# Keys and queries of three attention stages: loads moved from GpSimd's queue, with a cast, to SyncE's queue as plain float32, rows outermost

## The chip, the cores and the metric

One Trainium2 chip, one of its cores. The time is the device time of one execution in microseconds (us). Before the change the median of three runs is 3687.04 us (3684.84 to 3689.37).

## What is computed

Two transformer blocks on a sequence of 1024 rows of width 1024, all in float32. The first has latent attention (8 heads), dilated attention (8 heads) and a mixture of 16 experts; the second has two layers, each with differential attention (4 heads), grouped-query attention (6 heads over 2 key heads) and neighbourhood attention (6 heads), over 1024 grid rows and 256 context rows. Cut to what the change touches, which is the operands of the score products:

```python
def mla_attention(q, k, v):            # first block; k and q have 64 + 32 columns
    s = einsum('bqhd,bkhd->bhqk', q_blk, k) * scale
    return einsum('bhqk,bkhd->bqhd', softmax(s), v)
...
def dilated_branch(q, k, v, dilation, half):   # first block, three dilations
    s = einsum('brnqhd,brnkhd->brnhqk', qb, kb) * (Dh ** -0.5)
...
def second_block(...):                 # for each of 2 layers
    oa = diff_attend(qa, ka_all, va_all, lam)              # kind A
    yb = gqa_attend(qb, kb_all, vb_all) * silu(gb)         # kind B
    yn = neighbourhood_attend(qn, kn, vn, kn_c, vn_c, nat_rpb[l], rows) * silu(gn)   # kind C
    x = x + gt * (concatenate([ya, yb, yn]) @ w_out[l])
```

## The kernel before

TensorE multiplies float32 as sums of products of rounded parts: each operand is split into a high part and a rest, both of a type called float32r, which has the bits of a float32. The projections before an attention stage write their split, transposed queries and keys into HBM tensors `self.st[key]` ("stacks": Mk, Mq, Mr, Dk, Dq for the first block, Ak, Aq, Bk, Bq, Ck, Cq for a layer of the second). A stack is laid out as [part a (high, rest), block of heads, row, column], so a row of keys is 1024 or 1280 floats long (4 or 5 KB) and the two parts of a row lie far apart.

There are three attention stages: `attn1` (about 330 to 820 us of the profiled span), and `attn2` for layer 0 (about 2010 to 2570 us) and for layer 1 (about 3080 to 3570 us). In each a plan (`Plan`) simulates the engines ahead of time, with a cost for each operation written in the code, and issues operations in the order of the simulated time. An operation has a priority, a dictionary of the engines that may do it with its cost on each, the operations that it depends on and the buffers that it needs; it takes the first engine of the dictionary that is free. A load is such an operation: it takes the time given on the queue that issues it, and its data arrive after a modelled transfer. All instructions of an engine are chained in the order of the plan, those of SyncE (SP) alone are not (`Plan.issue`, lines 120 to 133). Every engine runs its instructions in order, and so does every queue that issues DMAs: an instruction that waits holds up what is behind it.

Two streams of heads are interleaved in each stage, so that TensorE (PE) has products of one while the softmax of the other runs on VectorE (DVE), ScalarE (ACT) and GpSimd (POOL). A stage's loads:

- keys: `mk` (latent), `ek` (dilated), `xk` (grouped-query and neighbourhood), `dk` (differential), two buffers each;
- queries: `mq`, `eq`, `xq` and `xx`, `dq` and `dx`, and `tb` for the rest of grouped-query queries;
- values `mv`, `ev`, `xv`, `dv`, gates `xg`, `dg`, tables of biases (`tb` from `c_rpb`), and in attn1 the weights `aw` of later modulations, 1 MB at a time: all of these are issued by SP already.

Keys and queries are issued by POOL. Their buffers are declared float32r and the stack float32, so each transfer is a cast. A key or query load has a priority `lead` before the first use of its head, so it can't start before the plan says so, nor before its buffer is free.

`Plan.early` (lines 143 to 153) issues the first few loads of a plan before the stage, while the projections still run; it hands the load the dictionary of engines in place of an engine's name.

The helpers of the loads are `ld_pair` (line 1869, two heads of queries), `ld_key` (line 1874, a head's keys, in both halves of the partitions) and `ld_maps` (line 1884, the differential head's 96 rows). In `ld_pair` the source's outermost dimension is the part (2), in `ld_key` it is a repeat of 2; in the latent loads (lines 964, 965, 976) and in line 2163 the rows are outermost:

```python
self.nc.gpsimd.dma_start(HL[:, a, :], bass.AP(tensor=src.tensor, offset=src.offset,
                         ap=[[0, 2]] + [list(x) for x in src.ap]))      # ld_key
nc.gpsimd.dma_start(K.t[:64], self.st["Mk"][:, p, 64*i:64*i+64, :].rearrange("a r c -> r a c"))
```

Of the kernel before, what the change touches and what calls it, by code (L numbers as in the profile page):

```python
# [9 lines left out]
F32 = mybir.dt.float32  # L10
# [215 lines left out]
class Kern:  # L226
# [722 lines left out]
    def mla_pair(self, p):  # L949
# [10 lines left out]
        def key(i):  # L960
            K = buf("mk", X, [100, 2, S], F32R)

            def ld(e):
                nc.gpsimd.dma_start(K.t[:64], self.st["Mk"][:, p, 64 * i:64 * i + 64, :].rearrange("a r c -> r a c"))
                nc.gpsimd.dma_start(K.t[64:100], self.st["Mr"][:, 0].rearrange("a r c -> r a c"))
            return K, pl.op(p0 - self.q["lead"], {"pool": 2.1}, ld, [], [K], 2.2)
        Ks = [key(i) for i in range(2)]

        def part(g):
# [3 lines left out]
            for i in range(2):  # L973
                K, lk = Ks[i]
                Q = buf("mq", X, [100, 2, 512], F32R)
                lq = pl.op(p0 - self.q["lead"] + 15 * i, {"pool": 1.05}, lambda e, Q=Q, i=i: nc.gpsimd.dma_start(
                    Q.t[:96], self.st["Mq"][:, 2 * p + i, :, g * 512:(g + 1) * 512].rearrange("a r c -> r a c")), [], [Q], 1.1)
# [92 lines left out]
    def dilated(self, dp):  # L1070
# [13 lines left out]
        for i in range(2):  # L1084
# [14 lines left out]
            for h in range(4 * i, 4 * i + 4):  # L1099
                p0 = self.at[X]  # L1100
                if h % 2 == 0:
                    Q = buf("eq", X, [P, 2, S], F32R)
                    lq = pl.op(p0 - self.q["lead"], {"pool": 2.1}, lambda e, Q=Q, h=h: self.ld_pair(Q.t, "Dq", h // 2, 0, S), [], [Q], 2.9)
                    loads.append(lq)
                K = buf("ek", X, [P, 2, S], F32R)
                lk = pl.op(p0 - self.q["lead"], {"pool": 2.1}, lambda e, K=K, h=h: self.ld_key(K.t, "Dk", h // 2, h % 2, False), [], [K], 2.9)
# [762 lines left out]
    def ld_pair(self, Q, key, blk, c0, n):  # L1869

        for i in range(2):
            self.nc.gpsimd.dma_start(Q[:, i, :], self.st[key][:, blk, 64 * i:64 * i + 64, c0:c0 + n])

    def ld_key(self, HL, key, blk, i, row):

        for a in range(2):
            src = self.st[key][a, blk, 64 * i:64 * i + 64, :]
            if a and row:
                self.nc.gpsimd.dma_start(HL[:64, a, :], src)
                self.pcopy(HL[64:68, a, :], self.ones[64:68].to_broadcast([4, S + 256]))  # L1880
                break
            self.nc.gpsimd.dma_start(HL[:, a, :], bass.AP(tensor=src.tensor, offset=src.offset, ap=[[0, 2]] + [list(x) for x in src.ap]))

    def ld_maps(self, A, key, h, c0, n):


        r0 = (h % 2) * 64
        for i in range(2):
            src = self.st[key][:, h // 2, r0 + 32 * i:r0 + 32 * i + 32, c0:c0 + n]
            if key == "Aq":  # L1890
                self.nc.gpsimd.dma_start(A[:64, i, :], src)
                self.nc.gpsimd.dma_start(A[64:96, i, :], src[0])
            else:
                s0 = src[0]
                self.nc.gpsimd.dma_start(A[:64, i, :], bass.AP(tensor=s0.tensor, offset=s0.offset, ap=[[0, 2]] + [list(x) for x in s0.ap]))
                self.nc.gpsimd.dma_start(A[64:96, i, :], src[1])
# [47 lines left out]
    def stream_d(self, l, with_ctx):  # L1944
# [25 lines left out]
        def head(h):  # L1970
# [4 lines left out]
            lk = pl.op(p0 - self.q["lead"], {"pool": 4.2}, lambda e: self.ld_maps(K.t, "Ak", h, 0, S + 256), [], [K], 2.7)  # L1975
# [3 lines left out]
            def group(g):  # L1979
                p0 = self.at[X]  # L1980
                Q = buf("dq", X, [96, 2, 512], F32R)
                lq = pl.op(p0 - self.q["lead"], {"pool": 4.2}, lambda e: self.ld_maps(Q.t, "Aq", h, g * 512, 512), [], [Q], 1.1)
# [22 lines left out]
                if g == 0 and with_ctx:  # L2005
                    Qx = buf("dx", X, [96, 2, 256], F32R)
                    lx = pl.op(p0 - self.q["lead"], {"pool": 4.2}, lambda e: self.ld_maps(Qx.t, "Aq", h, 2 * 512, 256), [], [Qx], 0.6)
# [108 lines left out]
    def stream_x(self, l, with_ctx):  # L2116
# [6 lines left out]
        def pair(kind, p):  # L2123
# [10 lines left out]
            for i, k in enumerate(ks):  # L2134
                if (kind, k) not in keys:
                    K = buf("xk", X, [P, 2, S + 256], F32R)
                    keys[kind, k] = K, pl.op(at - self.q["lead"] + 8 * i, {"pool": 2.1}, lambda e, K=K, k=k: self.ld_key(
# [359 lines left out]
```

## Time and profile before

| what | value |
|---|---|
| median of three runs | 3687.04 us |
| the profiled execution: its own time, its span | 3682.54 us, 3680.6 us |
| TensorE busy in the span | 3361.7 us (91%) |
| VectorE, ScalarE, GpSimd busy | 2352.2, 1710.7, 1205.9 us |
| mean granted clock of TensorE | 0.953 |
| chain of work that ended last | PE 55%, DVE 7%, DMA 7%, POOL 2%, ACT 2% |
| SP's DMA queue (q1) | 486.92 MB, 339828 packets |
| POOL's DMA queue (q0) | 94.63 MB, 160768 packets |

Times are those of one profiled execution. Instructions that issue DMAs aren't counted as busy time. A granted clock of 1.00 is TensorE at 2.4 GHz, 0.50 is 1.2 GHz. The DMA share is the mean busy share of the 16 DMA engines. A row of waits says who waited for whom, for how long in total, how many times, and the longest; where it says "issue", the engine waited for nothing that the profile shows.

### The profile page before, as it was taken

How to read it: one execution, taken by the hardware profiler on the slowest of the kernel's cores; microseconds unless marked ns; L12 is line 12 of the kernel's file. 1: busy time of each engine (PE TensorE's matmuls, PEld its weight loads, DVE VectorE, ACT ScalarE, POOL GpSimd, SP SyncE). 2: the span in 40 equal slices, each digit the busy share in tenths (PEclk: the TensorE clock that was granted, in tenths of full speed). 3: DMA queues.
4: the chain of work that ended last, by engine and by line, in shares of the span. 5: the costliest groups of instructions: out<-in, count | busy, mean ns of one | idle time of the engine just before them, and what ended most of it. 6: DMA issues, size and time to landing. Idle time of an engine off the chain costs nothing.

```text
span 3680.6 us, 51685 instructions
## 1 busy us (share of the span) xinstructions
PE 3361.7 (91%) x17880; PEld 2581.4 (70%) x17880; DVE 2352.2 (64%) x5558; ACT 1710.7 (46%) x3153; POOL 1205.9 (33%) x1069
## 2 busy tenths in 40 slices
PE   7998887889499999989999789999999999799999
PEld 5987555547388887779889555556899887465557
DVE  5525544444699998876841678887446814689962
ACT  4324444432288877653322566654333214565640
POOL 3111323232001001033530344565333512446661
PEclk9999898989699999989999899999999999899999
DMA  7348767666599999654452764213334445542133
GB/s 201 97 118 230 178 153 176 149 199 216 208 381 396 396 393 373 234 168 124 132 149 62 134 110 84 50 38 123 120 125 127 120 136 111 114 94 51 42 106 109
DMA packets 533178, 600.72 MB, mean 163 GB/s; under 512 B 203218, under 2 KB 409426, under 8 KB 528818
## 3 DMA queue, kind: packets, MB, share of 16 engines
q1 hardware_dynamic: 339828, 486.92, 40.2%
q0 software_dynamic: 160768, 94.63, 13.2%
q10 hardware_dynamic: 32320, 15.86, 1.6%
q8 instruction: 142, 2.33, 0.3%
q14 instruction: 120, 0.98, 0.1%
HBM read 473.33 MB, written 123.50 MB: 162 GB/s over the span
## 4 chain that ended last, share of the span: by engine, by line
PE 55%; DVE 7%; DMA 7%; POOL 2%; issue 2%; ACT 2%; SPq 0%; ACTq 0%; DVEq 0%; POOLq 0%
PE s L349 6%; PE s L350 6%; PE s L348 6%; PE a L350 6%; PE a L349 6%; PE a L348 6%; PE t L316 5%; PE o L1931 4%; DMA xk<-stackCk 3%; PE o L2226 2%; PE s L2027 2%; PE s L2186 1%; PE s L2269 1%; DMA xk<-stackBk 1%; PE t L1939 1%
## 5 line engine op out<-in xcount | busy, mean ns | idle before, releaser
L348 PE MATMUL a<-wh,h2H 128*128 128x384 f32 (+2 forms) x1328 | 477.1, 359 | 8.2 <-ACT vd L1608 5.0
L350 PE MATMUL a<-wh,h2L 128*128 128x384 f32 (+2 forms) x1328 | 470.3, 354 | 3.6 <-POOL h2L L596 3.6
L349 PE MATMUL a<-wl,h2H 128*128 128x384 f32 (+2 forms) x1328 | 469.9, 354 | 1.3 <-DVE wl L335 1.3
L1481 DVE TENSOR_TENSOR wl<-wr,wh 128x1024 fp32r<-128x1024 f32 x384 | 450.4, 1221 | 25.9 <-ACT wh L1480 19.2
L1480 ACT ACTIVATE wh<-wr 128x1024 fp32r<-128x1024 f32 x384 | 395.9, 1059 | 77.3 <-PE s L350 74.7
L348 PEld LDWEIGHTS a<-wh,h2H 128*128 128x128 f32 x1328 | 252.5, 190 | 30.0 <-ACT vd L1608 5.4
L350 PEld LDWEIGHTS a<-wh,h2L 128*128 128x128 f32 x1328 | 252.2, 190 | 27.1 <-POOL h2L L596 5.0
L349 PEld LDWEIGHTS a<-wl,h2H 128*128 128x128 f32 x1328 | 252.6, 190 | 22.7 <-DVE wl L335 1.6
L1861 DVE CUSTOM_DVE_ANT_0 dP<-s,zero 128x512 f32<-128x512 f32 (+1 forms) x384 | 218.0, 595 | 23.2 <-PE s L2027 22.1
L349 PE MATMUL s<-wl,xH 128*128 128x512 f32 x512 | 201.5, 394 | 4.5 <-DVE wl L1481 4.2
L348 PE MATMUL s<-wh,xH 128*128 128x512 f32 x512 | 202.2, 395 | 0.0
L350 PE MATMUL s<-wh,xL 128*128 128x512 f32 x512 | 199.8, 390 | 0.0
L2049 ACT ACTIVATE dP<-dP,d 128x1280 f32<-128x1280 f32 x128 | 174.2, 1363 | 44.2 <-DVE d L2043 41.0
L1057 POOL TENSOR_TENSOR xP<-xP,xPT 128x512 f32<-128x512 f32 x130 | 181.8, 1398 | 36.1 <-DVE xP L1057 12.5
L1020 DVE TENSOR_REDUCE x<-s 128x1 f32<-128x512 f32 (+1 forms) x240 | 157.2, 683 | 22.2 <-PE s L2186 21.6
L348 PE MATMUL s<-wh,yoH 128*128 128x512 f32 x416 | 166.6, 402 | 1.5 <-DVE yo L2406 0.8
L349 PE MATMUL s<-wl,yoH 128*128 128x512 f32 x416 | 165.8, 399 | 0.8 <-DVE wl L335 0.8
L350 PE MATMUL s<-wh,yoL 128*128 128x512 f32 x416 | 164.6, 396 | 0.0
L1053 ACT ACTIVATE xPT<-t 128x512 f32<-128x512 f32 x240 | 130.0, 604 | 72.9 <-PE t L2191 63.5
L335 POOL TENSOR_TENSOR wl<-wr,wh 128x1024 fp32r<-128x1024 f32 (+3 forms) x43 | 93.9, 2183 | 209.9 <-ACT wh L333 205.7
L2269 PE MATMUL s<-xk,xq 128*128 128x512 f32 (+2 forms) x480 | 106.9, 341 | 47.8 <-issue 30.9
L1463 POOL DMA_INDIRECT xg<-h2d,idx x16 | 16.4, 1027 | 400.8 <-PE t L316 326.5
(456 smaller groups left out, 8355.6 us busy)
## 6 DMA issues: line engine op xcount, KB each, us to landing
wr<-in_w_gate_dram SPq DMA_DIRECT2D x128, 512.0 KB
wr<-in_w_up_dram SPq DMA_DIRECT2D x128, 512.0 KB
wr<-in_w_down_dram SPq DMA_DIRECT2D x128, 512.0 KB
aw<-in_w_ada_dram SPq DMA_DIRECT2D x32, 1024.0 KB
wr<-in_w_in_dram SPq DMA_DIRECT2D x44, 512.0 KB
aw<-in_w_ada_dram SPq DMA_DIRECT2D x32, 512.0 KB
xk<-stackCk POOLq DMA_DIRECT2D x24, 640.0 KB, 23.6
wr<-in_w_in_dram SPq DMA_DIRECT2D x36, 384.0 KB
```

What stands on the lines that cost most here:

```text
L316: self.nc.tensor.transpose(out, in_, self.ident[:n, :n])
L348: nc.tensor.matmul(out, sH, h, start=first, stop=False)
L349: nc.tensor.matmul(out, sH, l, start=False, stop=False)
L350: nc.tensor.matmul(out, sL, h, start=False, stop=last)
L1020: nc.vector.tensor_reduce(dst, Sb.t[:, :n * w].rearrange("p (k c) -> p k c", k=n) if n > 1 else Sb.t[:, :w], AX.X, ALU.max)
L1057: eng.tensor_tensor(A.t[:, :512], PT.t[:, 0, :] if kb == 1 else A.t[:, :512], PT.t[:, kb, :], ALU.add)
L1480: nc.scalar.activation(h, raw, AF.Copy)
L1481: nc.vector.tensor_tensor(l, raw, h.bitcast(F32), ALU.subtract)
L1861: self.nc.vector.tensor_tensor_reduce(dst, src, self.zero.to_broadcast(list(src.shape)), 1.0, -3e38, ALU.add, ALU.max, m)
L1931: nc.tensor.matmul(O.t[a * 64:(a + 1) * 64, :], v(kb), PT[0](kb), start=(kb < 2), stop=(kb >= nb - 2))
L2049: nc.scalar.activation(Ps[i].t, Ps[i].t, AF.Exp, bias=b["m"][:, i:i + 1], accum_out=box[j][:, i:i + 1])
L2269: nc.tensor.matmul(Sb[a].t[:, c:c + n], q, K.t[:, h, lo * P + k0:lo * P + k0 + n], start=(h == 0), stop=(h == 1))
```

## The change

Every load of split keys and queries goes through a new helper `fetch`. It issues the transfer from SP if the plan chose the engine "sp", else from POOL, and it declares the destination as float32, so nothing is cast. In the plan the loads' engine is now "sp" with 0.45 to 1.3 us in place of "pool" with 1.05 to 4.2 us. Loads that `Plan.early` issues go to POOL as before, without the cast. The three helpers make the rows the outermost dimension of every transfer: a pair of queries is still two transfers, a key still two (one for each half of the partitions, both parts in each), a differential load three in place of four.

```diff
--- before.py
+++ after.py
@@ -961,9 +961,9 @@
             K = buf("mk", X, [100, 2, S], F32R)
 
             def ld(e):
-                nc.gpsimd.dma_start(K.t[:64], self.st["Mk"][:, p, 64 * i:64 * i + 64, :].rearrange("a r c -> r a c"))
-                nc.gpsimd.dma_start(K.t[64:100], self.st["Mr"][:, 0].rearrange("a r c -> r a c"))
-            return K, pl.op(p0 - self.q["lead"], {"pool": 2.1}, ld, [], [K], 2.2)
+                self.fetch(e, K.t[:64], self.st["Mk"][:, p, 64 * i:64 * i + 64, :].rearrange("a r c -> r a c"))
+                self.fetch(e, K.t[64:100], self.st["Mr"][:, 0].rearrange("a r c -> r a c"))
+            return K, pl.op(p0 - self.q["lead"], {"sp": 0.9}, ld, [], [K], 2.2)
         Ks = [key(i) for i in range(2)]
 
         def part(g):
@@ -973,8 +973,8 @@
             for i in range(2):
                 K, lk = Ks[i]
                 Q = buf("mq", X, [100, 2, 512], F32R)
-                lq = pl.op(p0 - self.q["lead"] + 15 * i, {"pool": 1.05}, lambda e, Q=Q, i=i: nc.gpsimd.dma_start(
-                    Q.t[:96], self.st["Mq"][:, 2 * p + i, :, g * 512:(g + 1) * 512].rearrange("a r c -> r a c")), [], [Q], 1.1)
+                lq = pl.op(p0 - self.q["lead"] + 15 * i, {"sp": 0.45}, lambda e, Q=Q, i=i: self.fetch(
+                    e, Q.t[:96], self.st["Mq"][:, 2 * p + i, :, g * 512:(g + 1) * 512].rearrange("a r c -> r a c")), [], [Q], 1.1)
 
                 def s1(j, c0, w, dst, Q=Q, K=K):
                     nc.tensor.matmul(dst, Q.t[:96, 0, j * P:(j + 1) * P], K.t[:96, 0, c0:c0 + w], start=True, stop=True)
@@ -1100,10 +1100,10 @@
                 p0 = self.at[X]
                 if h % 2 == 0:
                     Q = buf("eq", X, [P, 2, S], F32R)
-                    lq = pl.op(p0 - self.q["lead"], {"pool": 2.1}, lambda e, Q=Q, h=h: self.ld_pair(Q.t, "Dq", h // 2, 0, S), [], [Q], 2.9)
+                    lq = pl.op(p0 - self.q["lead"], {"sp": 0.9}, lambda e, Q=Q, h=h: self.ld_pair(e, Q.t, "Dq", h // 2, 0, S), [], [Q], 2.9)
                     loads.append(lq)
                 K = buf("ek", X, [P, 2, S], F32R)
-                lk = pl.op(p0 - self.q["lead"], {"pool": 2.1}, lambda e, K=K, h=h: self.ld_key(K.t, "Dk", h // 2, h % 2, False), [], [K], 2.9)
+                lk = pl.op(p0 - self.q["lead"], {"sp": 0.9}, lambda e, K=K, h=h: self.ld_key(e, K.t, "Dk", h // 2, h % 2, False), [], [K], 2.9)
                 loads.append(lk)
                 for part in "BA":
                     for half in range(2):
@@ -1866,34 +1866,29 @@
     def put_y(self, t_, t0, n, c0, w):
         self.nc.scalar.dma_start(self.yd[t0 * P:(t0 + n) * P, c0:c0 + w].rearrange("(t p) c -> p t c", p=P), t_)
 
-    def ld_pair(self, Q, key, blk, c0, n):
-
-        for i in range(2):
-            self.nc.gpsimd.dma_start(Q[:, i, :], self.st[key][:, blk, 64 * i:64 * i + 64, c0:c0 + n])
-
-    def ld_key(self, HL, key, blk, i, row):
+    def fetch(self, e, dst, src):
+
+        (self.nc.sync if e == "sp" else self.nc.gpsimd).dma_start(dst.bitcast(F32), src)
+
+    def ld_pair(self, e, Q, key, blk, c0, n):
 
         for a in range(2):
-            src = self.st[key][a, blk, 64 * i:64 * i + 64, :]
-            if a and row:
-                self.nc.gpsimd.dma_start(HL[:64, a, :], src)
-                self.pcopy(HL[64:68, a, :], self.ones[64:68].to_broadcast([4, S + 256]))
-                break
-            self.nc.gpsimd.dma_start(HL[:, a, :], bass.AP(tensor=src.tensor, offset=src.offset, ap=[[0, 2]] + [list(x) for x in src.ap]))
-
-    def ld_maps(self, A, key, h, c0, n):
+            self.fetch(e, Q[64 * a:64 * a + 64], self.st[key][a, blk, :, c0:c0 + n].rearrange("(i r) c -> r i c", i=2))
+
+    def ld_key(self, e, HL, key, blk, i, row):
+
+        src = self.st[key][:, blk, 64 * i:64 * i + 64, :].rearrange("a r c -> r a c")
+        self.fetch(e, HL[:64], src)
+        self.fetch(e, HL[64:, :1] if row else HL[64:], src[:, :1] if row else src)
+        if row:
+            self.pcopy(HL[64:68, 1, :], self.ones[64:68].to_broadcast([4, S + 256]))
+
+    def ld_maps(self, e, A, key, h, c0, n):
 
 
         r0 = (h % 2) * 64
-        for i in range(2):
-            src = self.st[key][:, h // 2, r0 + 32 * i:r0 + 32 * i + 32, c0:c0 + n]
-            if key == "Aq":
-                self.nc.gpsimd.dma_start(A[:64, i, :], src)
-                self.nc.gpsimd.dma_start(A[64:96, i, :], src[0])
-            else:
-                s0 = src[0]
-                self.nc.gpsimd.dma_start(A[:64, i, :], bass.AP(tensor=s0.tensor, offset=s0.offset, ap=[[0, 2]] + [list(x) for x in s0.ap]))
-                self.nc.gpsimd.dma_start(A[64:96, i, :], src[1])
+        for b, a in enumerate((0, 1, 0) if key == "Aq" else (0, 0, 1)):
+            self.fetch(e, A[32 * b:32 * b + 32], self.st[key][a, h // 2, r0:r0 + 64, c0:c0 + n].rearrange("(i r) c -> r i c", i=2))
 
     def trans_ops(self, p, stream, dep, Pt, blocks, PT, dst):
 
@@ -1972,14 +1967,14 @@
             K = buf("dk", X, [96, 2, S + 256], F32R)
             V = buf("dv", X, [P, 10, 64])
             Y, G_ = buf("dy", X, [P, 10, 64]), buf("dg", X, [P, 10, 64])
-            lk = pl.op(p0 - self.q["lead"], {"pool": 4.2}, lambda e: self.ld_maps(K.t, "Ak", h, 0, S + 256), [], [K], 2.7)
+            lk = pl.op(p0 - self.q["lead"], {"sp": 1.3}, lambda e: self.ld_maps(e, K.t, "Ak", h, 0, S + 256), [], [K], 2.7)
             lv = pl.op(p0 - self.q["lead"], {"sp": 0.1}, lambda e: self.part_cols(V.t, "A", 0, 10, h * 64, 64), [], [V], 0.9)
             fins = []
 
             def group(g):
                 p0 = self.at[X]
                 Q = buf("dq", X, [96, 2, 512], F32R)
-                lq = pl.op(p0 - self.q["lead"], {"pool": 4.2}, lambda e: self.ld_maps(Q.t, "Aq", h, g * 512, 512), [], [Q], 1.1)
+                lq = pl.op(p0 - self.q["lead"], {"sp": 1.3}, lambda e: self.ld_maps(e, Q.t, "Aq", h, g * 512, 512), [], [Q], 1.1)
                 PT = buf("dPT", X, [P, 10, 4, P])
                 box = {}
                 evs = []
@@ -2004,7 +1999,7 @@
                                            lambda kb: V.t[:, kb, :], [PT, V], fin))
                 if g == 0 and with_ctx:
                     Qx = buf("dx", X, [96, 2, 256], F32R)
-                    lx = pl.op(p0 - self.q["lead"], {"pool": 4.2}, lambda e: self.ld_maps(Qx.t, "Aq", h, 2 * 512, 256), [], [Qx], 0.6)
+                    lx = pl.op(p0 - self.q["lead"], {"sp": 1.3}, lambda e: self.ld_maps(e, Qx.t, "Aq", h, 2 * 512, 256), [], [Qx], 0.6)
                     for gq in range(2):
                         fins.append(self.d_ctx(self.step(X, 1.0), gq, Qx, K, V, Y, [lx, lk, lv], coeff, combine, sm))
             for g in range(2):
@@ -2134,8 +2129,8 @@
             for i, k in enumerate(ks):
                 if (kind, k) not in keys:
                     K = buf("xk", X, [P, 2, S + 256], F32R)
-                    keys[kind, k] = K, pl.op(at - self.q["lead"] + 8 * i, {"pool": 2.1}, lambda e, K=K, k=k: self.ld_key(
-                        K.t, part + "k", k // 2, k % 2, kind == "B"), [], [K], 3.6)
+                    keys[kind, k] = K, pl.op(at - self.q["lead"] + 8 * i, {"sp": 0.9}, lambda e, K=K, k=k: self.ld_key(
+                        e, K.t, part + "k", k // 2, k % 2, kind == "B"), [], [K], 3.6)
                     loads.append(keys[kind, k][1])
             K = [keys[kind, k] for k in ks]
             TB = [None, None]
@@ -2151,7 +2146,7 @@
                 n = 2 if g == 2 else 4
                 Q, G_, Y = (buf(a + "x" if g == 2 else b, X, [P] + sh, dt) for a, b, sh, dt in (
                     ("x", "xq", [2, n * P], F32R), ("xg", "xg", [n, P], F32), ("xy", "xy", [n, P], F32)))
-                lq = pl.op(at - self.q["lead"], {"pool": 2.1}, lambda e: self.ld_pair(Q.t, part + "q", p, g * 512, n * P), [], [Q], 1.5)
+                lq = pl.op(at - self.q["lead"], {"sp": 0.9}, lambda e: self.ld_pair(e, Q.t, part + "q", p, g * 512, n * P), [], [Q], 1.5)
                 loads.append(lq)
                 lg = pl.op(at - self.q["lead"], {"sp": 0.1}, lambda e: self.part_cols(G_.t, part, 4 * g, n, g0 + p * P, P), [], [G_], 0.7)
                 if g == 2:
@@ -2160,8 +2155,8 @@
                     fins = [self.nat_group(g, i, Q, K[i], TB[i], V, vcol[i], Y, G_, [lq, lv, lg], sm) for i in range(2)]
                 else:
                     Qm = buf("tb", X, [68, 2, 512], F32R)
-                    lm = pl.op(at - self.q["lead"], {"pool": 1.05}, lambda e: nc.gpsimd.dma_start(
-                        Qm.t[:64], self.st["Bq"][0, p, :, g * 512:(g + 1) * 512].rearrange("(i r) c -> r i c", i=2)), [], [Qm], 0.7)
+                    lm = pl.op(at - self.q["lead"], {"sp": 0.45}, lambda e: self.fetch(
+                        e, Qm.t[:64], self.st["Bq"][0, p, :, g * 512:(g + 1) * 512].rearrange("(i r) c -> r i c", i=2)), [], [Qm], 0.7)
                     fins = [self.gqa_group(i, Q, Qm, K[i], V, vcol[i], Y, G_, [lq, lv, lg, lm], sm) for i in range(2)]
                 pl.op(self.at[X], {"act": 0.1}, lambda e: self.put_y(Y.t, 4 * g, n, y0 + p * P, P), fins, [Y], 0.7)
             for g in (0, 2, 1) if with_ctx else (0, 1):
```

## Rows read from the trace of the kernel before

**Rows 1.** stages: span; busy PE, PEld, DVE, ACT, POOL; clock; DMA share; GB/s

```profile
330.00:820.00 490.00, 409.77 (x2381) 269.70 (x2380) 237.45 (x628) 205.96 (x546) 149.75 (x141) 0.89 0.69 173
2010.00:2570.00 560.00, 504.50 (x2765) 322.53 (x2764) 442.85 (x1285) 324.07 (x659) 285.79 (x285) 0.93 0.44 91
3080.00:3570.00 490.00, 450.84 (x2475) 279.67 (x2473) 396.09 (x1194) 288.94 (x537) 278.50 (x259) 0.97 0.40 85
```

**Rows 2.** waits of PE in attn1: total us, times, longest

```profile
PE s L1150 <- issue: 20.9, 2, 10.6
PE s L980 <- DMA mq<-stackMq: 16.5, 4, 10.0
PE s L467 <- DMA aw<-in_w_ada_dram: 15.9, 2, 8.3
PE s L980 <- issue: 7.7, 1, 7.7
```

**Rows 3.** waits of PE in layer 0's attention

```profile
PE s L2269 <- DMA xk<-stackCk: 14.4, 3, 11.3
PE s L2269 <- issue: 11.5, 1, 11.5
PE o L2226 <- DMA xv<-partC: 10.1, 1, 10.1
PE t L316 <- ACT oT L1855: 5.6, 1, 5.6
```

**Rows 4.** waits of PE in layer 1's attention

```profile
PE s L2269 <- issue: 19.4, 3, 10.1
PE s L2186 <- DMA xk<-stackBk: 3.2, 1, 3.2
```

**Rows 5.** timeline of PE, two stalls: start, duration, in brackets idle before

```profile
529.24 2.24 PE L1150 MATMUL s<-ek,eq 128*128 128x256 f32 x8 [10.30 <-issue]
2085.02 0.77 PE L2269 MATMUL s<-xk,xq 128*128 128x512 f32 x1 [11.53 <-issue]
```

**Rows 6.** timeline of POOL: three loads as it issues them

```profile
508.75 1.58 POOL L1882 DMA_DIRECT2D ek<-stackDk  x2
2061.01 1.63 POOL L1882 DMA_DIRECT2D xk<-stackCk  x2 [0.28 <-issue]
2283.00 0.66 POOL L1895 DMA_DIRECT2D dk<-stackAk  x1 [10.16 <-DMA xk<-stackBk]
```

**Rows 7.** DMA issues: out<-in, count, KB each, median us from issue to landing

```profile
ek<-stackDk POOLq DMA_DIRECT2D x16, 512.0 KB, 21.1
mk<-stackMk POOLq DMA_DIRECT2D x8, 512.0 KB, 7.2
xk<-stackCk POOLq DMA_DIRECT2D x24, 640.0 KB, 23.6
```

**Rows 8.** windows: weights alone in the experts' stage; a key's two transfers alone

```profile
1100.00:1500.00 400.00, 397.35 (x1832) 326.64 (x1832) 371.56 (x364) 315.50 (x333) 36.97 (x22) 1.00 1.02 387
3122.00:3131.00 9.00, 9.00 (x62) 6.04 (x60) 6.94 (x28) 7.16 (x14) 3.17 (x2) 1.00 0.29 105
```

**Rows 9.** windows right after twelve stalls: the first, the ninth and the last

```profile
372.00:382.00 10.00, 9.55 (x42) 5.76 (x42) 6.16 (x12) 1.96 (x4) 0.00 (x0) 0.67 1.26 201
...
2288.00:2320.00 32.00, 28.01 (x87) 16.95 (x88) 25.50 (x62) 18.28 (x34) 18.50 (x15) 0.65 0.33 73
...
3291.00:3301.00 10.00, 9.08 (x47) 5.89 (x47) 6.56 (x17) 3.13 (x9) 4.96 (x4) 0.83 0.72 117
```

**Rows 10.** waits of SP's queue over the span

```profile
SPq L1864 <- POOL xy L2175: 464.0, 19, 60.4
SPq L463 <- PE s L467: 282.8, 33, 21.5
SPq L2145 <- DVE x L1861: 84.7, 4, 27.1
```

**Rows 11.** lines of POOL in layer 0's attention: count, busy, mean ns, idle before

```profile
L1057 POOL TENSOR_TENSOR xP<-xP,xPT 128x512 f32<-128x512 f32 x55 | 75.7, 1376 | 23.4 <-DVE xP L1057 9.9 <-ACT xPT L1053 6.2 <-ACT dPT L1855 1.9
```

## Prediction

> **What bounds the kernel now.** I read the page first: TensorE is busy for 91% of the span, so only a stretch where it stands still can give much, and DMA holds 7% of the chain that ended last. The only such stretches that the change touches are the three attention stages. Windows over them [rows 1] show PE idle for 490 - 409.8 = 80 us in attn1, 560 - 504.5 = 56 us in layer 0 and 490 - 450.8 = 39 us in layer 1, with DVE, ACT and POOL each busy for less than PE. The reader should see that PE sets the pace and that 175 us of standing still is the most that could be won there, slow clock apart.
>
> PE's waits stage by stage say what it stood still for. In attn1 they name mq outright, and "issue" before products of ek and mk [rows 2]; in the second block xk, twice by name and four times as "issue" [rows 3, 4]. I take "issue" here for the same wait, because the timeline of PE has each of these in front of the first product that reads a new key. That is 20.9 + 16.5 + 7.7 = 45.1 us, 14.4 + 11.5 = 25.9 us, and 19.4 + 3.2 = 22.6 us. One wait of 5.6 us is put down to ACT [rows 3], but comes from POOL: it stood 10.16 us at a load of dk until an earlier transfer had landed, with additions of the softmax queued behind [rows 6]. I count it too: 99.2 us.
>
> Next, why they are late. POOL issued the ek that PE missed at 508.75 [rows 6]; PE stopped at 529.24 - 10.30 = 518.9 [rows 5]: 10.2 us were allowed. The xk went out at 2061.01, right when its buffer came free, and PE stopped at 2085.02 - 11.53 = 2073.5: 12.5 us were allowed. But ek takes a median of 21.1 us to land and xk 23.6 [rows 7]. Issuing earlier isn't possible without another buffer; landing faster is.
>
> **The change part by part.** *Shape of the transfers.* The row that decides is mk: the same 512 KB as ek, on the same queue with the same cast, lands in 7.2 us [rows 7]; its rows are outermost, ek's repeat of 2 is. Where a key's two transfers run nearly alone, they move 105 GB/s with under a third of the 16 engines busy, while the weights get 387 GB/s with all of them [rows 8]. So two 640 KB transfers need 1.31 MB / 105 = 12.5 us now and 1.31 / 387 = 3.4 us with all engines. For the fixed part I take mk's landing less its bytes at that rate, 7.2 - 1.4 = 5.8 us (an upper bound, its wait for other transfers included): 9.2 us for a key, against 12.5 allowed. A pair of dilated queries with a key is 2.1 MB: 5.4 + 5.8 = 11.2 against 10.2, so 1 us stays, and 2.7 us more where 1 MB of aw is ahead in the same queue. I keep 7 us of the 99 for two such places: -92. Bounds: 0, if landing stays above 23 us; -99.
>
> The Trainium skill, "DMA: Bandwidth & Descriptors", section "Issuing engines are not separate DMA queues", speaks against the change: transfers from any queue end on the same 16 engines, so another issuer saves only the time to issue. By it alone the sum would be the 5.6 us that POOL's blocked issue cost; by the rows it is what the shape gives. It returns as a rival below.
>
> *The clock behind the stalls.* After each stall TensorE runs with a lower granted clock, 0.67 in the first stretch, 0.65 in the longest, 0.83 in the last of twelve [rows 9]. Busy time times one less clock is what it costs: 9.55 x 0.33 = 3.2 us in the first, 28.01 x 0.35 = 9.8 in the ninth, 9.08 x 0.17 = 1.5 in the last, 37 us in all. Half of the ninth I leave out, since other waits stand in that stretch; of the 32 left I take 30, as the stalls go but for 7 us. Bounds 0 and -37.
>
> *Other transfers.* Three stalls are for loads that SP issued all along: xv 10.1 us [rows 3], aw 15.9 us [rows 2], in stretches crowded with the loads in question. If those pass at 387 in place of 105 GB/s, the crowd thins, but now they share a queue with them. I take -6 of 26; bounds 0 and -26.
>
> *Issue on POOL.* Some 250 issues leave POOL, at 0.65 to 0.8 us each [rows 6]. None is on the path but the one counted, so 0. Its cover is PE, busy for longer than POOL in each stage [rows 1].
>
> *The plan.* By the costs in the code, some 120 us of POOL's planned time in layer 0 come free (keys 16.8, queries of x 37.8, tb 6.3, differential 67.2, less what goes early), some 90 in layer 1, 50 in attn1. Operations with a choice take the first free engine, POOL, so more additions and combinations go from DVE to it. DVE isn't the bound and POOL has room on average [rows 1]: 0, bounds -8 and +56 (below).
>
> *SP's queue.* Every load now stands in one queue with SP's own waits. It waits for POOL's gated product before a gate can be loaded (24 us in the mean, up to 60.4), for PE before the next aw (8.6 in the mean, up to 21.5), for DVE before a table (up to 27.1) [rows 10]. Behind such an instruction stand keys and queries, and PE waits for those. Both old and new order follow the events by which buffers come free, so most of these waits end before the next key's buffer does. I take four places with 5 us each, half of the 10 us allowed: +20, clock included. The bounds are 0 and the third rival.
>
> Sum: -92 - 30 - 6 + 20 = -108 us. The profiled execution took 3682.5 us (2 us around its span), so 3574.5; the median of the runs is 4.5 us above it, which gives **3579 us**.
>
> **The rivals.**
> 1. *The engines, not the shape.* In the crowded stretches all 16 engines may have been the limit, and the landing shortens by half only. The Trainium skill's rule above points the same way. For: attn1 has a DMA share of 0.69 in the mean [rows 1] and 1.26 behind its first stall [rows 9]. Against: mk against ek, and 105 GB/s with no crowd. Half of the 122: 3687 - 61 + 5 = 3631.
> 2. *POOL becomes the bound.* An addition takes 1376 ns there [rows 11] where the plan reckons 0.6 us on DVE; a chain of nine ends 7 us later. If one in three of the 24 grouped-query groups shows it, +56: 3635. For: POOL is at 278 of 490 us in layer 1 without its issues [rows 1]. Against: mostly hidden behind the other stream.
> 3. *SP's queue takes the wait, and it is slower.* In attn1, 24 groups of latent loads come to stand behind aw. With the longest wait, 21.5 us [rows 10], and 2.7 us for the 1 MB ahead, less 10 us allowed, one costs 14 us. It decides from nine such groups on, which eat the gain; at twelve, +170 - 108 = +62: 3749. For: SP's order isn't chained to the plan. Against: aw is freed by PE itself, in PE's order, as are the keys' buffers.
> 4. *Nothing.* The loads are issued later by as much as they land sooner: 3687.
>
> **How the numbers follow.** The forecast has 0.60, rival 1 0.14, rival 2 0.12, rival 3 0.08, rival 4 0.06. This kernel can tell 0.2% (7 us) from no change: faster 0.86, same 0.06, slower 0.08. At the fast end everything counted goes, 99 + 37 + 26 + 8 = 170: 3517. At the slow end rivals 1 and 2 stand at 3631 and 3635, each some 15 us wide: 3650. Outside lie the last two rivals and some of the tails. The forecast's own range is 3525 to 3615.
>
> **What would show it.** Right: xk and ek on SP's queue, landing in under 10 us; no wait of PE over 4 us for xk, ek, mq; a granted clock near 1.00 through the stages; attn1 some 45 us shorter, layer 0 some 35, layer 1 some 25; POOL's queue down from 94.6 MB to under 30. Wrong: landing times still near 20 us (rival 1); PE waiting for additions of POOL late in each layer (rival 2); rows of SP that wait with keys late behind them, and PE stalls of over 10 us in new places (rival 3).

## The result: 3584 us, and the profile after

The changed kernel takes 3584.08 us in the median of four runs (3579.02 to 3594.27), the kernel before, run beside it, 3687.24: a ratio of 0.9724 (0.9702 to 0.9746), 103 us less. The forecast was 3579. The profiled span is 3577.2 us, 103.4 below that of before.

From the page of the changed kernel, TensorE's busy time and two DMA queues (packets, MB, share of 16 engines' span):

```profile
PE 3347.1 (94%) x17880; PEld 2582.2 (72%) x17880; DVE 2323.2 (65%) x5516; ACT 1702.3 (48%) x3122; POOL 1149.4 (32%) x885
...
q1 hardware_dynamic: 367284, 554.83, 48.9%
q0 software_dynamic: 6944, 26.22, 3.0%
```

PE does the same 17880 products in a shorter span. POOL's queue carries 26.2 MB: the early loads, 9.4 MB by the sizes in the list of DMA issues, and the indirect transfers of the experts' stage, which the change leaves as they were. Its packets fall from 160768 to 6944.

Windows of the changed kernel over attn1, layer 0 and layer 1, cut where the stages now lie (columns as in [rows 1]):

```profile
330.00:787.00 457.00, 410.34 (x2347) 272.10 (x2344) 224.29 (x597) 198.08 (x517) 151.34 (x119) 0.91 0.65 183
1976.70:2488.80 512.10, 488.56 (x2689) 306.43 (x2688) 430.82 (x1269) 316.50 (x642) 264.61 (x197) 0.96 0.36 90
3013.60:3454.80 441.20, 425.24 (x2410) 271.86 (x2412) 377.84 (x1175) 285.35 (x534) 235.84 (x180) 0.98 0.37 88
```

PE stands still for 46.7, 23.5 and 16.0 us; in the kernel before it was 80.2, 52.8 and 36.6 us between the same marks. To compare kernels stage by stage I use marks that each trace has: attn1 ends when SP loads the gate behind it (line 527), a layer's attention runs from the first product of xq and xk to the load of its gate. Before: 817.9, 542.5 and 474.9 us. After: 787.1, 512.1 and 441.2. So attn1 gave 31 us, layer 0 30, layer 1 34, and 8 came from between attn1 and layer 0, which no step had named.

Waits of PE in the changed kernel, in attn1 and then in layer 0 (total us, times, longest):

```profile
PE s L980 <- DMA mq<-stackMq: 23.1, 12, 5.8
...
PE s L2022 <- DMA xg<-partC: 3.2, 1, 3.2
```

No wait for xk or ek is left, and neither the aw of [rows 2] nor the xv of [rows 3]. The wait for mq is 23.1 us, in twelve pieces; before it was 16.5 us, or 24.2 with the 7.7 us put down to "issue" before the same product [rows 2]. In layer 1 a wait of 4.7 us for a differential query (`dq`) is new. DMA issues of the changed kernel:

```profile
xk<-stackCk SPq DMA_DIRECT2D x16, 640.0 KB
...
xk<-stackCk POOLq DMA_DIRECT2D x8, 640.0 KB, 11.3
```

SP's issues show no landing time. The eight early transfers of keys, which POOL still issues, land in 11.3 us; POOL's transfers of xk in [rows 7] took 23.6.

### The profile page after: what moved, and what is told of

Same layout as the page of the kernel before. It is cut to its first block, busy times and chain, and to the rows that moved or that the text cites. A ratio compares the mean times of both kernels' runs of the same rounds, so it can differ in the third digit from the quotient of the medians.

```text
span 3577.2 us, 51580 instructions
## 1 busy us (share of the span) xinstructions
PE 3347.1 (94%) x17880; PEld 2582.2 (72%) x17880; DVE 2323.2 (65%) x5516; ACT 1702.3 (48%) x3122; POOL 1149.4 (32%) x885
## 5 line engine op out<-in xcount | busy, mean ns | idle before, releaser
L1057 POOL TENSOR_TENSOR xP<-xP,xPT 128x512 f32<-128x512 f32 x138 | 197.1, 1428 | 42.3 <-DVE xP L1057 14.2
L2044 ACT ACTIVATE dP<-dP,d 128x1280 f32<-128x1280 f32 x128 | 174.2, 1364 | 39.8 <-DVE d L2038 36.6
L1855 ACT ACTIVATE oT<-o 128x512 f32<-128x512 f32 (+2 forms) x96 | 45.7, 477 | 233.9 <-PE o L1926 111.2
L335 DVE TENSOR_TENSOR wl<-wr,wh 128x1024 fp32r<-128x1024 f32 (+3 forms) x55 | 70.2, 1277 | 119.9 <-ACT wh L333 119.9
```

What stands on the lines that cost most here:

```text
L335: e.tensor_tensor(l, raw, h.bitcast(F32), ALU.subtract)
L1057: eng.tensor_tensor(A.t[:, :512], PT.t[:, 0, :] if kb == 1 else A.t[:, :512], PT.t[:, kb, :], ALU.add)
L2044: nc.scalar.activation(Ps[i].t, Ps[i].t, AF.Exp, bias=b["m"][:, i:i + 1], accum_out=box[j][:, i:i + 1])
```

## The experiments

Four theories stood against each other. *Shape*: rows outermost is the gain. *Issuer*: SP and the missing cast are. *Plan*: the new costs in the plan change the order on the engines, for better or worse. *SP's queue*: loads stand behind SP's own waits and 1 MB of aw, which costs. The change has three switches (the shape; the issuing queue, and with it the cast; the plan), and the runs set them one by one. Each was timed beside the kernel before on the same chip, on two chips in all; the medians of the kernel before lie between 3683 and 3691 us. (The trace calls POOL's queue POOLq and SP's SPq.)

**Rows outermost alone**, issued by POOL with the cast, old plan:

```diff
-        (self.nc.sync if e == "sp" else self.nc.gpsimd).dma_start(dst.bitcast(F32), src)
+        self.nc.gpsimd.dma_start(dst, src)
...
-            return K, pl.op(p0 - self.q["lead"], {"sp": 0.9}, ld, [], [K], 2.2)
+            return K, pl.op(p0 - self.q["lead"], {"pool": 2.1}, ld, [], [K], 2.2)
```

The other nine loads get their old costs back in the same way.

> One part alone: the three helpers put the rows outermost, as in the changed kernel; the loads stay with POOL, with the cast, at the plan's old costs. Theory 'shape' (a transfer's outermost dimension sets on how many engines it runs, and so when it lands): xk and ek land in under 12 us in place of 23.6 and 21.1, PE's long waits for them go, and most of the gain is there: about 3610 us. Rival 'issuer' (what cost was POOL as issuer, with its cast and its place in POOL's order): landing stays near 20 us, the time within 15 us of 3687.

3557.36 us, ratio 0.964 (0.9624 to 0.9656): 134 us less than before (3691.46 in this set), more than the whole change. Its DMA issues (median us to landing last):

```profile
q0 software_dynamic: 34880, 94.13, 12.7%
...
xk<-stackCk POOLq DMA_DIRECT2D x24, 640.0 KB, 10.1
...
ek<-stackDk POOLq DMA_DIRECT2D x16, 512.0 KB, 14.1
...
eq<-stackDq POOLq DMA_DIRECT2D x8, 512.0 KB, 9.4
...
mk<-stackMk POOLq DMA_DIRECT2D x8, 512.0 KB, 6.0
```

The same bytes from the same queue need 34880 packets in place of 160768, and xk lands in 10.1 us, not 23.6. mk, whose shape was right already, lands in 6.0 (7.2). Shape holds; issuer falls. Two expectations were missed: ek, at 14.1 us, stays above 12, and the gain is larger than I had put it.

**Rows outermost and plain**, issued by POOL, old plan (as above, but `dst.bitcast(F32)` stays).

> Rows outermost and plain float32 as in the changed kernel, but planned on and issued by POOL at the old costs. Against rows alone it takes only the cast away; against the changed kernel it has another queue and the old plan. 'Shape': keys land in 6 to 10 us, time 3580 to 3600; and if loads that stand behind aw in SP's queue are what attn1 still waits for (PE waits for mq: 23.1 us in 12 waits there), these waits fall below 12 us and the time is at or below that of the changed kernel, 3584. 'Issuer': POOL's blocked issues still hold up its additions, 3630 or more.

3564.55 us, ratio 0.9661 (0.9644 to 0.9678). The cast cost nothing that can be measured: without it the ratio is 0.002 higher, and the two intervals overlap. PE waits 10.0 us for mq and the time lies below the changed kernel's, as the theory of SP's queue wanted. A window of this run, in layer 1, with a key's two transfers nearly alone (the last three columns are clock, DMA share, GB/s):

```profile
3113.00:3118.00 5.00, 5.00 (x37) 3.73 (x37) 4.49 (x16) 4.85 (x9) 1.43 (x3) 1.00 0.97 219
```

The old shape had a share of 0.29 and 105 GB/s there [rows 8]. So on POOL's queue too the shape decides how much of the engines is used.

**Queue and plan without the shape**: SP, plain, new plan, old access patterns.

```diff
-        for a in range(2):
-            self.fetch(e, Q[64 * a:64 * a + 64], self.st[key][a, blk, :, c0:c0 + n].rearrange("(i r) c -> r i c", i=2))
+        for i in range(2):
+            self.fetch(e, Q[:, i, :], self.st[key][:, blk, 64 * i:64 * i + 64, c0:c0 + n])
...
```

(`ld_pair`; the other two helpers get their old access patterns back in the same way.)

> The other part alone: loads planned on and issued by SP as plain float32, with the old shapes (outermost dimension 2 or a repeat of 2). Theory 'shape': a key's two transfers still run at some 105 GB/s, 12.5 us of bytes and some 17 us in all, so each key still misses by 5 to 10 us, and other loads stand behind it in SP's queue: 3650 us or more. Rival 'issuer': the time is that of the changed kernel within 15 us, 3570 to 3600.

3998.07 us, ratio 1.0834 (1.0811 to 1.0856): 307 us slower than before. By the issuer theory it had to be 3570 to 3600. PE waits 131.3 us for mq and 85.0 for xk.

**The plan alone**: new costs, but before's transfers, with the cast, issued by POOL.

```diff
-        (self.nc.sync if e == "sp" else self.nc.gpsimd).dma_start(dst.bitcast(F32), src)
+        self.nc.gpsimd.dma_start(dst, src)
...
-        for a in range(2):
-            self.fetch(e, Q[64 * a:64 * a + 64], self.st[key][a, blk, :, c0:c0 + n].rearrange("(i r) c -> r i c", i=2))
+        for i in range(2):
+            self.fetch(e, Q[:, i, :], self.st[key][:, blk, 64 * i:64 * i + 64, c0:c0 + n])
...
```

> Only the plan's view: loads cost SP's time in the plan, as in the changed kernel, but are issued by POOL with the cast and the old shapes. 'Shape': no gain, and a plan that no longer knows of POOL's load issues, so 3680 to 3720. Rival 'plan' (the gain comes from more additions on POOL and another order): 3640 or less.

3757.6 us, ratio 1.019 (1.0169 to 1.0211): 66 us slower than before, worse than either side had it. The order that the new plan makes doesn't help by itself. Here it also takes POOL's time to issue for free, which it isn't; the next runs part the two.

**The new plan with the new shape, issued by POOL** (the fetch of the changed kernel without its choice of SP):

```diff
-        (self.nc.sync if e == "sp" else self.nc.gpsimd).dma_start(dst.bitcast(F32), src)
+        self.nc.gpsimd.dma_start(dst.bitcast(F32), src)
```

> The changed kernel with its plan as it is (the loads are planned on SP), plain float32 and rows outermost, but every one of these loads is issued by GpSimd. If the plan's order is what costs the changed kernel its 20 us against rows outermost alone, this stays at 3580 us or above (GpSimd's issue time is now unplanned as well). If SP's queue costs it, the time falls to that of rows outermost on GpSimd, 3557 to 3565 us, with waits for mq of about 10 us in all.

3623.06 us, ratio 0.9828 (0.9778 to 0.9878). Without SP's queue the kernel is 39 us slower still, and the waits for mq are 33.5 us. That speaks against SP's queue as what costs the changed kernel its 20 us, but doesn't settle it, for POOL must now issue what the plan left out of POOL's time.

**The old plan with the new shape, issued by SP** (the ten old costs, and the choice made by whether the load is early):

```diff
-        (self.nc.sync if e == "sp" else self.nc.gpsimd).dma_start(dst.bitcast(F32), src)
+        (self.nc.gpsimd if isinstance(e, dict) else self.nc.sync).dma_start(dst.bitcast(F32), src)
...
-            return K, pl.op(p0 - self.q["lead"], {"sp": 0.9}, ld, [], [K], 2.2)
+            return K, pl.op(p0 - self.q["lead"], {"pool": 2.1}, ld, [], [K], 2.2)
```

> Plain float32 and rows outermost, the loads of the stages issued by SP as in the changed kernel, but the plan keeps the old costs on GpSimd. If SP's queue costs the changed kernel its 20 us, this is at 3580 to 3590 us with waits for mq of over 20 us. If the plan's order does, this falls to 3557 to 3565 us.

3554.25 us, ratio 0.9637 (0.9592 to 0.9681). The SP-queue theory, which was mine, falls; the plan theory holds. Since the two kernels had not been timed side by side, both went to one chip, with five rounds:

> The changed kernel itself, beside the next kernel on the same chip. If the plan's new costs are what it loses, it is 15 to 30 us slower than the next kernel, 12 to 15 of them in layer 0; if the difference between the earlier runs came from the chips, the two agree within 8 us.

> The changed kernel with the plan's old costs on GpSimd, but issued by SP, again, on the same chip as the changed kernel. By the plan theory 3550 to 3565 us, 15 to 30 us below the changed kernel; by the rival the same within 8 us.

The changed kernel: 3581.13 us (3569.89 to 3591.43), ratio 0.9733 (0.971 to 0.9757). With the old costs: 3551.25 us (3543.63 to 3557.53), ratio 0.965 (0.9628 to 0.9672). The intervals lie apart: ten numbers of the plan cost 30 us.

**SP and plain alone**: old shapes, old plan; early loads stay with POOL. Against the kernel before:

```diff
+        (self.nc.gpsimd if isinstance(e, dict) else self.nc.sync).dma_start(dst.bitcast(F32), src)
...
-            self.nc.gpsimd.dma_start(HL[:, a, :], bass.AP(tensor=src.tensor, offset=src.offset, ap=[[0, 2]] + [list(x) for x in src.ap]))
+            self.fetch(e, HL[:, a, :], bass.AP(tensor=src.tensor, offset=src.offset, ap=[[0, 2]] + [list(x) for x in src.ap]))
...
```

The other loads go through `fetch` in the same way.

> The kernel before with its transfers issued by SP as plain float32 and nothing else: old shapes, old plan. If SP's queue costs nothing whatever the shape, this is at 3687 us. If the old shapes are worse on SP's queue than on GpSimd's, as the run with the new plan (3998 us against 3758 us) suggests, it is at 3850 us or above, with waits of PE for mq and xk that add up to over 100 us.

3957.94 us, ratio 1.0749 (1.0723 to 1.0775): 275 us slower. PE waits for xk 79.7 us and for mq 66.8, and mq's own shape is the same in all of these kernels. How it comes to wait is in the timeline of SP (start, duration) around one such stall:

```profile
713.19 18.24 SPq L1871 DMA_DIRECT2D ek<-stackDk  x2
731.53 9.75 SPq L463 DMA_DIRECT2D aw<-in_w_ada_dram  x1
741.39 1.00 SPq L1871 DMA_DIRECT2D mq<-stackMq  x1
```

and in the same kernel's timeline of PE:

```profile
762.78 2.47 PE L980 MATMUL s<-mk,mq 96*128 96x512 f32 x5 [29.46 <-DMA mq<-stackMq]
```

Two issues of ek hold SP for 18.24 us (1.53 in the changed kernel, below), aw goes out after them and mq after that, and PE stands for 29.5 us. Windows over this stretch (the last three columns are clock, DMA share, GB/s):

```profile
715.00:725.00 10.00, 6.47 (x32) 4.45 (x30) 0.42 (x1) 6.25 (x16) 3.85 (x3) 1.00 0.12 50
725.00:735.00 10.00, 8.04 (x36) 3.99 (x36) 3.48 (x11) 2.56 (x9) 3.82 (x3) 0.83 0.13 53
735.00:745.00 10.00, 0.00 (x0) 0.00 (x0) 0.00 (x0) 0.00 (x0) 0.00 (x0) 0.58 0.39 119
745.00:755.00 10.00, 0.00 (x0) 0.00 (x0) 0.00 (x0) 0.00 (x0) 0.00 (x0) 0.50 0.72 185
755.00:763.00 8.00, 0.22 (x1) 0.25 (x2) 0.00 (x0) 0.00 (x0) 0.00 (x0) 0.50 0.13 52
```

The reader should see 0.12 to 0.13: two of sixteen engines, at 50 to 53 GB/s. In the trace's records of packets, two are under way at once for 95% of the first and of the last window. In between, more engines work, while SP has issued aw and mq; then two are left until mq has landed. That a part of mq stood behind ek on these two is how I read it; the trace doesn't name the engines. On POOL's queue the same shape had 0.29 and 105 GB/s [rows 8].

**The keys' shape alone**: `ld_key` with rows outermost, all else as before.

```diff
-            self.nc.gpsimd.dma_start(HL[:, a, :], bass.AP(tensor=src.tensor, offset=src.offset, ap=[[0, 2]] + [list(x) for x in src.ap]))
+        src = self.st[key][:, blk, 64 * i:64 * i + 64, :].rearrange("a r c -> r a c")
+        self.nc.gpsimd.dma_start(HL[:64], src)
+        self.nc.gpsimd.dma_start(HL[64:, :1] if row else HL[64:], src[:, :1] if row else src)
...
```

> The kernel before with one helper changed: the keys of ek and xk have rows outermost; pairs of queries and the differential loads keep their old shape, GpSimd issues everything, with the cast and the old plan. The theory that the stalls for late keys are the loss expects landing of xk near 10 us and of ek near 14 us, the stalls for xk and ek gone, and two thirds of what rows outermost gave in all: 3600 to 3620 us. The rival, that it is the load of the whole queue (all of the small packets) and not the keys' own landing, expects less than a third: 3645 us or above.

3640.75 us, ratio 0.9878 (0.9828 to 0.9927): 43 us, a third of the shape's gain and near the rival. Its DMA issues:

```profile
xk<-stackCk POOLq DMA_DIRECT2D x24, 640.0 KB, 13.7
ek<-stackDk POOLq DMA_DIRECT2D x16, 512.0 KB, 25.0
...
eq<-stackDq POOLq DMA_DIRECT2D x8, 512.0 KB, 23.6
```

and its waits of PE in attn1:

```profile
PE s L1150 <- DMA eq<-stackDq: 18.5, 2, 12.3
PE s L1150 <- issue: 11.5, 1, 11.5
```

ek, in its good shape, lands in 25.0 us in the median. One by one in the trace, the ten transfers issued right behind a pair of queries in the old shape land in 21.5 to 39.4 us, the four issued alone after 450 us in 5.4 to 12.5; two issued alone at 359 us, among many other loads, take 24.0 and 25.7. attn1 is no shorter (818.5), layer 0 gains 17 us and layer 1 20. A key is only as early as the slowest load beside it, so the shape pays when all of them have it.

**attn1's loads back to POOL**, planned there, in the changed kernel:

```diff
-            return K, pl.op(p0 - self.q["lead"], {"sp": 0.9}, ld, [], [K], 2.2)
+            return K, pl.op(p0 - self.q["lead"], {"pool": 2.1}, ld, [], [K], 2.2)
```

> The changed kernel, but in attn1 alone keys and queries are planned on and issued by GpSimd again (plain float32, rows outermost); both layers are as changed. The SP-queue theory (a latent query stands behind 1 MB of aw and a pair of dilated loads in one queue) expects attn1 about 8 us shorter than in the changed kernel, as with rows outermost on GpSimd, waits for mq down from 23 us to 10 us, the layers unchanged, and about 3575 us. The rival, that what the changed kernel loses comes from the plan's new costs in the layers or from noise of the order, expects attn1 unchanged within 2 us and 3584 us.

3580.46 us, ratio 0.9708 (0.9663 to 0.9752). Waits for mq fell to 9.2 us as my theory said, but attn1 ended at 790.6, not earlier. Up to the end of attn1 its instructions stand in the same order on PE, DVE, POOL and SP as in the rows-and-plain run on POOL, which ended attn1 at 778.8. What differs most is a stall in the timeline of PE here:

```profile
576.64 1.94 PE L467 MATMUL s<-aw,cs 128*32 128x512 f32 x8 [8.37 <-DMA aw<-in_w_ada_dram]
```

and the same product there:

```profile
567.49 1.07 PE L467 MATMUL s<-aw,cs 128*32 128x512 f32 x8 [1.59 <-DMA aw<-in_w_ada_dram]
```

So attn1 alone varies by 12 us from execution to execution, and 6.8 of the 12 are this wait for one megabyte of aw. This run decides nothing about attn1.

All of them by stage, in us of the profiled span (end of attn1; the two layers from first product to gate):

| shape | issued by | plan | attn1 ends | layer 0 | layer 1 | median |
|---|---|---|---|---|---|---|
| old | POOL | old (before) | 817.9 | 542.5 | 474.9 | 3687 |
| old | POOL | new | 854.5 | 568.3 | 486.5 | 3758 |
| old | SP | old | 917.6 | 626.4 | 565.7 | 3958 |
| old | SP | new | 937.1 | 653.7 | 553.2 | 3998 |
| rows | POOL, cast | old | 779.3 | 498.8 | 442.7 | 3557 |
| rows | POOL | old | 778.8 | 499.5 | 441.6 | 3565 |
| rows | POOL | new | 805.4 | 531.3 | 445.5 | 3623 |
| rows | SP | old, twice | 774.0, 764.5 | 498.5, 497.8 | 444.5, 445.1 | 3554, 3551 |
| rows | SP | new (changed), twice | 787.1, 784.7 | 512.1, 513.0 | 441.2, 439.0 | 3584, 3581 |
| rows | POOL in attn1, then SP | old in attn1, then new | 790.6 | 515.9 | 439.8 | 3580 |
| keys only | POOL, cast | old | 818.5 | 525.4 | 454.5 | 3641 |

## Why the prediction came out right, and where its steps did not

**The shape: -92, -30 and -6, together -128.** Right, in mechanism and size. With the old plan the shape gives 134 (POOL, cast), 127 (POOL, plain), 129 and 132 us (SP), each against the kernel before beside it. By parts: between the marks of the three stages PE stood still for 169.6 us before and was busy for 1335.7. In the four profiled executions with rows outermost and the old plan it stands still for 89 to 99 us less (forecast 92 + 6) and is busy for 20 to 29 us less (forecast 30). The waits of PE for xk and ek that I counted, those put down to "issue" among them, are gone from the changed kernel. mk was fast and ek slow because the old shape leaves engines idle: on SP's queue it used two of the sixteen, and on POOL's the share rose from 0.29 to 0.97 with rows outermost. How many engines one transfer had on POOL's queue, no run shows. The Trainium skill, "DMA: Bandwidth & Descriptors", section "Why a DMA increments its semaphore by 16 and not by 1", has a rule that fits: a transfer is spread over the largest number of engines, up to 16, that divides the outermost dimension of both sides, and on a hardware queue they are the lowest-numbered ones; a 2 there gives two engines, and the share of 0.13 agrees. Rival 1 (the sixteen engines were the limit) is out: they were idle for want of being used. One figure was off: I reckoned 387 GB/s for a key with all engines, and it was 219 with a share of 0.97, so its 1.31 MB take 6.0 us, not 3.4. By an estimate with that rate the fixed part is shorter (7.2 - 2.4 = 4.8 us, not 5.8) and a key takes 10.8 us; xk landed in 10.1, against the 9.2 that I had reckoned.

**The size of single stages was off.** I had attn1 at -45, layer 0 at -35, layer 1 at -25; the changed kernel shows -31, -30 and -34, and 8 between attn1 and layer 0. Of these 8, 6 to 7 go with the shape of the keys: from the first store of the projections' values (line 1609) to the first product it takes 423 to 425 us in the four kernels with the old keys and 417 to 420 in the nine with rows outermost, the one with the keys alone included.

**SP's in-order queue: +20.** Wrong: 0. On SP, with the old plan, the kernel is as fast as on POOL (3554 and 3551 against 3557 and 3565; ratios 0.9637 and 0.965 against 0.964 and 0.9661). The wait itself exists. In the changed kernel, the timeline of SP in attn1:

```profile
487.25 1.24 SPq L1871 DMA_DIRECT2D eq<-stackDq  x2
488.53 1.53 SPq L1871 DMA_DIRECT2D ek<-stackDk  x2
492.32 0.34 SPq L463 DMA_DIRECT2D aw<-in_w_ada_dram  x1
495.29 0.34 SPq L1871 DMA_DIRECT2D mq<-stackMq  x1
```

and the product that follows, in the timeline of PE:

```profile
506.02 2.50 PE L980 MATMUL s<-mk,mq 96*128 96x512 f32 x5 [4.93 <-DMA mq<-stackMq]
```

3 MB stand ahead of mq, and PE stops for 4.9 us. The longest of the twelve stops for mq are 5.8, 4.9, 3.8 and 2.1 us, near the four of 5 that I forecast. But it is the new plan that brings them, on either queue: with rows outermost the waits for mq are 23.1 us (SP) and 33.5 (POOL) with the new plan, and 9.2 to 15.9 in the five runs that have the old one in attn1. Nor does SP's queue cost more in all: waits for mq and aw together are 29.0 and 24.1 us on POOL with the old plan, 15.1 and 19.5 on SP with the old plan, 23.1 in the changed kernel, where no wait for aw is left. Rival 3 has its mechanism at a third of the price that it needed.

**The plan: 0, with bounds -8 and +56.** Wrong, and it is the step that failed: +30, by the two kernels on one chip, inside the bounds but not near 0. That the forecast, 3579, came within 5 us is luck: this error and the last one cancel. By stage the new plan costs 20 us in attn1 and 15 in layer 0, and gives back 6 in layer 1 (profiled executions on one chip). Windows over attn1 and layer 0, changed kernel on that chip:

```profile
330.00:784.70 454.70, 408.00 (x2335) 270.69 (x2335) 222.47 (x596) 197.41 (x516) 151.05 (x118) 0.91 0.65 184
1978.20:2491.20 513.00, 489.71 (x2688) 308.29 (x2688) 431.01 (x1269) 316.07 (x641) 264.80 (x197) 0.95 0.35 90
```

The same two with the old costs:

```profile
330.00:764.50 434.50, 393.77 (x2335) 257.98 (x2334) 234.60 (x619) 202.89 (x540) 114.06 (x89) 0.94 0.68 192
1955.20:2453.00 497.80, 479.73 (x2689) 302.32 (x2687) 435.12 (x1276) 320.62 (x654) 209.89 (x168) 0.97 0.36 92
```

The products are as many, but for one, yet PE is busy 14 and 10 us longer, at a clock of 0.91 and 0.95 in place of 0.94 and 0.97, and idle 6 and 5 us longer. I had foreseen what the plan does: POOL's work in the two stages goes from 114 and 210 us to 151 and 265. In the lines of POOL, over the span, of the changed kernel:

```profile
L1961 POOL TENSOR_TENSOR dP<-dP,dP 128x1280 f32<-128x1280 f32 x43 | 126.7, 2948 | 3.6
L1057 POOL TENSOR_TENSOR mA<-mA,mPT 128x512 f32<-128x512 f32 x94 | 121.8, 1296 | 27.1 <-ACT mPT L1053 12.9 <-DVE mA L1057 7.4
```

and with the old costs:

```profile
L1057 POOL TENSOR_TENSOR mA<-mA,mPT 128x512 f32<-128x512 f32 x65 | 84.9, 1307 | 49.0 <-DVE mA L1057 30.0 <-ACT mPT L1053 9.3 <-DVE e L1165 3.7
L1961 POOL TENSOR_TENSOR dP<-dP,dP 128x1280 f32<-128x1280 f32 x26 | 76.3, 2933 | 2.2
```

17 more combinations and 29 more additions go to POOL. But POOL, at 265 of 513 us, is not the bound that rival 2 made of it, and no large wait of PE for POOL appears. The price comes in small stops. In layer 0 PE stops for over 0.6 us 14 times in each of the three profiled executions with the new plan and SP's queue there, at a clock of 0.95 to 0.96, and 7 times in each of the four with rows outermost and the old plan, at 0.97. One that stands alike in those three, from the timeline of PE of the changed kernel:

```profile
2332.98 1.05 PE L316 MATMUL t<-ident,dP 128*128 128x128 f32 x4 [1.92 <-DVE tb L1042]
2334.90 0.69 PE L316 MATMUL t<-ident,dP 128*128 128x128 f32 x2 [0.87 <-DVE d L1861]
...
2336.91 1.98 PE L1926 MATMUL o<-xPT,xv 128*64 128x512 f32 x4
```

and DVE in the same stretch:

```profile
2329.86 2.35 DVE L1057 TENSOR_TENSOR xP<-xP,xPT 128x512 f32<-128x512 f32 x2
2332.24 0.68 DVE L1042 TENSOR_TENSOR tb<-t,ident 4x512 fp32r<-4x512 f32 x1
```

PE stops for 1.9 and 0.9 us, since what it needs stands behind additions on DVE, and then four products of line 1926 take 1.98 us, where four took 1.08 at 2327.61, before the stop; the granted clock is 0.51 from 2335.6 to 2340, the lower of its two levels. That the new order brings such stops, and that the lower clock carries most of the loss (10 of 15 us, as busy time), is shown for layer 0, where every run with the new plan is 13 us or more above its partner with the old one. Which of the plan's decisions make them isn't: it was not tried to change one at a time. In attn1 the difference of 20 us has the 12 us of chance within it.

**Issue on POOL: 0.** Right while the plan reckons with it (3565 against 3554 and 3551); 40 us where the plan leaves it out (3623 against 3584 and 3581).

**Clock and the waits to be seen.** The mean clock rose from 0.953 to 0.965, POOL's queue fell to 26 MB, no stall of PE for xk or ek is left. Two signs failed: mq still stops PE for up to 5.8 us, over the 4 I had named, and the clock in attn1 is 0.91, not near 1.00. The landing of keys on SP's queue can't be read, since SP's issues show none.

## What to carry to other kernels

Look first at which dimension of a transfer is outermost and at the DMA share while it runs alone: a share of 0.13 at 50 GB/s is a shape, not a busy memory, and it can be mended without touching the queue, for all the loads that share it. A planner's costs are part of the kernel: when an edit makes an operation free in the plan, everything that fills the gap moves, so time the edit with the old costs too. Here the changed transfers with the old costs take 3551 us, and rows outermost alone, one edit of three helpers, can't be told from it (ratios 0.965 and 0.964).

## What was unexpected on the hardware

The same transfers with an outermost dimension of 2 are far worse on SP's hardware queue (share 0.12 to 0.13, 50 to 53 GB/s) than on POOL's (0.29, 105 GB/s), and there SP itself is held, 18.24 us for two issues, with everything behind it. Why the two queues differ, no run shows. With rows outermost a key keeps the engines busy (0.97) at 219 GB/s, while the weights got 387 with a share of 1.02 [rows 8]: a share near 1 isn't yet the highest rate. The float32r cast on POOL's queue, which I had never priced, costs nothing that can be measured: 3557 us with it and 3565 without.
